# A row softmax over 4096 x 32768 values: the hardware loop turned by half a step

## The chip, the cores and the metric

One core of a Trainium2 chip. The time is that of one execution on the device in microseconds (us); lower is better. Medians are over several executions, and kernels of one comparison ran in turn on the same chip. Engines are named as in the profile: DVE is the vector engine, ACT the scalar engine, SP the sync engine (here it issues every transfer), PE the matrix engine (idle here); SPq and PEq are the instruction streams of SP and PE. In the kernels before and after, L75 and L83 are the lines of the file that issue a load and a store, and L115 is the first work of a tile, the max.

## The reference, cut to what matters

```python
logits = randn(16, 256, 32768).astype(float32); temperature = 1.0
scaled = logits / temperature
scaled = scaled - scaled.max(axis=-1, keepdims=True)
e = exp(scaled)
return e / e.sum(axis=-1, keepdims=True)          # float32
```

4096 rows of 128 KiB are read once and written once: 537 MB each way.

## The kernel before

Each row is cut in two halves on two neighbouring partitions, so a tile is 128 half rows of 16384 values (8.39 MB), and there are 64 tiles. Three tile buffers are used in turn. `normalise` does all arithmetic of a tile in place (four pieces of 4096 columns: max on DVE, exp on ACT, then the scaling on both). There is one chunk per tile (C = 1), and `turn` is None outside the loop. A step is one tile: normalise tile i, store it, load tile i+2 into the buffer that tile i-1 has left. Steps 0 to 2 are written out, steps 3 to 59 are a hardware loop of 19 turns of three steps, steps 60 to 63 are written out.

```python
_BUFS = 3                       # G = n_chunks = 64, C = 1
# ... cut: load, store, combine, pieces, normalise ...
    def step(i, turn=None, per_turn=0):
        g, c = divmod(i, C)
        end = turn is None and g == G - 1
        if c == 0:
            normalise(g, _END_PIECE if end else _PIECE)
        store(i, _END_DMA if end else CW, turn, per_turn)
        j = i + _BUFS - 1
        if i and j < n_chunks:
            end = turn is None and j // C == G - 1
            load(j, _END_DMA if end else CW, turn, per_turn)

    per_turn = 3
    first = per_turn
    turns = (n_chunks - (_BUFS - 1) - C - first) // per_turn      # 19
    with tc.manual_schedule():
        for i in range(_BUFS):
            load(i, _END_DMA if i < C else CW)
        for i in range(first):
            step(i)
        with tc.For_i(0, turns, 1, iteration_sync="reg_based") as turn:
            for i in range(first, first + per_turn):
                step(i, turn, per_turn)
        for i in range(first + turns * per_turn, n_chunks):
            step(i)
```

Of the kernel before, what the change touches and what calls it, by code (L numbers as in the profile page):

```python
# [11 lines left out]
_PIECE = 4096  # L12
_END_DMA = 4096
_END_PIECE = 4096
# [5 lines left out]
def kernel(  # L20
# [20 lines left out]
    C = W // CW  # L41
# [3 lines left out]
    G = N * _SPLIT // P  # L45
# [17 lines left out]
    def spans(total: int, step: int) -> list[tuple[int, int]]:  # L63
        return [(s, min(step, total - s)) for s in range(0, total, step)]

    def rows(i: int, turn, per_turn: int):
        g = i // C
        if turn is None:
            return slice(g * P, (g + 1) * P)
        return bass.ds(turn * (per_turn // C * P) + g * P, P)  # L70

    def load(i: int, step: int, turn=None, per_turn: int = 0) -> None:
        c = i % C
        for s, n in spans(CW, step):
            nc.sync.dma_start(  # L75
                out=buf[i % _BUFS][:, s : s + n],
                in_=x[rows(i, turn, per_turn), c * CW + s : c * CW + s + n],
            )

    def store(i: int, step: int, turn=None, per_turn: int = 0) -> None:  # L80
        c = i % C
        for s, n in spans(CW, step):
            nc.sync.dma_start(  # L83
                out=o[rows(i, turn, per_turn), c * CW + s : c * CW + s + n],
                in_=buf[i % _BUFS][:, s : s + n],
            )

    def combine(v, op) -> None:
        for j in range(n_rounds):
            mask = [i ^ (1 << j) for i in range(32)]  # L90
            nc.vector.stream_shuffle(  # L91
                out=v[:, j + 1 : j + 2], in_=v[:, j : j + 1], mask=mask
            )
            nc.vector.tensor_tensor(  # L94
                out=v[:, j + 1 : j + 2],
                in0=v[:, j : j + 1],
                in1=v[:, j + 1 : j + 2],
                op=op,
            )

    def pieces(g: int, step: int):
        k = 0
        for c in range(C):
            xs = buf[(g * C + c) % _BUFS]
            for s, n in spans(CW, step):
                yield k, xs[:, s : s + n], n
                k += 1

    def normalise(g: int, step: int) -> None:
        st = stat[g % _SETS]  # L110
        K = W // step
        nm, ssum, ee, f, ttj = (st[k][:, :K] for k in ("nm", "ssum", "ee", "f", "ttj"))
        nMh, Sh, rS = st["nMh"], st["Sh"], st["rS"]
        for k, xc, n in pieces(g, step):
            nc.vector.tensor_reduce(  # L115
                out=nm[:, k : k + 1], in_=xc, axis=X, op=A.max, negate=True
            )
            if inv_t != 1.0:
                nc.vector.tensor_scalar_mul(
                    out=nm[:, k : k + 1], in0=nm[:, k : k + 1], scalar1=inv_t  # L120
                )
            nc.scalar.activation(  # L122
                out=xc,
                in_=xc,
                func=Exp,
                bias=nm[:, k : k + 1],
                scale=inv_t,
                accum_out=ssum[:, k : k + 1],
            )
        nc.vector.tensor_reduce(out=nMh[:, 0:1], in_=nm, axis=X, op=A.min)  # L130
        combine(nMh, A.min)
        nc.scalar.activation(  # L132
            out=ee, in_=nm, func=Exp, bias=nMh[:, n_rounds : n_rounds + 1], scale=-1.0
        )
        nc.vector.tensor_tensor_reduce(  # L135
            out=ttj,
            in0=ee,
            in1=ssum,
            scale=1.0,
            scalar=0.0,  # L140
            op0=A.mult,
            op1=A.add,
            accum_out=Sh[:, 0:1],
        )
        combine(Sh, A.add)
        nc.vector.reciprocal(out=rS, in_=Sh[:, n_rounds : n_rounds + 1])  # L146
        nc.vector.tensor_scalar_mul(out=f, in0=ee, scalar1=rS)  # L147
        for k, xc, n in pieces(g, step):
            cut = int(n * _DVE_SHARE) // 512 * 512
            nc.vector.tensor_scalar_mul(  # L150
                out=xc[:, :cut], in0=xc[:, :cut], scalar1=f[:, k : k + 1]
            )
            nc.scalar.activation(  # L153
                out=xc[:, cut:], in_=xc[:, cut:], func=Copy, scale=f[:, k : k + 1]
            )

    def step(i: int, turn=None, per_turn: int = 0) -> None:
        g, c = divmod(i, C)
        end = turn is None and g == G - 1
        if c == 0:  # L160
            normalise(g, _END_PIECE if end else _PIECE)
        store(i, _END_DMA if end else CW, turn, per_turn)
        j = i + _BUFS - 1
        if i and j < n_chunks:
            end = turn is None and j // C == G - 1
            load(j, _END_DMA if end else CW, turn, per_turn)

    per_turn = 3
    first = per_turn
# [3 lines left out]
    with tc.manual_schedule():  # L173
        for i in range(_BUFS):
            load(i, _END_DMA if i < C else CW)
        for i in range(first):
            step(i)
        with tc.For_i(0, turns, 1, iteration_sync="reg_based") as turn:
# [4 lines that stand above are left out]
# [35 lines left out]
```

## Time and profile before

| | before |
|---|---|
| time, median of 4 runs | 2520.2 us (2519.25 to 2520.98) |
| span of the profiled run | 2519.8 us |
| DVE busy, ACT busy | 63%, 54% |
| transfer queue, share of 16 engines | 98.6% |
| GB/s inside the loop (200 to 2300 us) | 434 |
| GB/s in slice 38 of 40 | 224 |
| DVE's wait at the barrier of the loop's exit | 49.3 us |

How to read it: the row that is near 100% is the transfer queue (98.6%; the engines are at 63% and 54%), so I take an engine's idle time here to matter only where it holds up a transfer. The place to look for is where the rate falls, and there is one, just before the end. The profile's lines on it stand in the prediction.

### The profile page before, as it was taken

The numbers are of one execution on the slowest core, as the hardware profiler recorded it, in microseconds if no ns is written. First come the engines' busy times: TensorE is split into PE (matmuls) and PEld (weight loads), VectorE is DVE, ScalarE is ACT, GpSimd is POOL, SyncE is SP. The second block draws the span as 40 slices with busy tenths as digits, with TensorE's granted clock in tenths as the row PEclk, the third lists the DMA queues.
The fourth block names the chain that finished last, engine by engine and source line by source line (L and its number), as shares of the span: only waits on it lengthen the run. The fifth ranks groups of instructions, "written<-read, shape, count | busy, mean of one in ns | idle before, by whom it ended". The sixth has DMA issues, their size and how long they took to land. (4 is left out here: it accounts for less than half of the span.)

```text
span 2519.8 us, 4389 instructions
## 1 busy us (share of the span) xinstructions
DVE 1579.6 (63%) x1216; ACT 1368.7 (54%) x833; POOL 0.2 (0%) x4
## 2 busy tenths in 40 slices
DVE  6576565665766656657666666576566665765375
ACT  5464554655645546456455465464554654645255
POOL 0000000000000000000000000000000000000000
DMA  9999999999999999999999999999999999999599
GB/s 416 433 433 433 429 435 431 432 428 432 433 437 436 433 433 434 433 433 433 435 434 435 434 438 435 433 434 433 433 433 434 435 436 433 435 436 436 224 398 402
DMA packets 19733, 1073.79 MB, mean 426 GB/s; under 512 B 2192, under 2 KB 2192, under 8 KB 2192
## 3 DMA queue, kind: packets, MB, share of 16 engines
q1 hardware_dynamic: 19728, 1073.75, 98.6%
q14 instruction: 5, 0.04, 0.0%
HBM read 536.87 MB, written 536.87 MB: 426 GB/s over the span
## 5 line engine op out<-in xcount | busy, mean ns | idle before, releaser
L115 DVE TENSOR_REDUCE nm<-x 128x1 f32<-128x4096 f32 x256 | 1113.7, 4412 | 677.0 <-DMA x<-in_logits_dram 627.7
L122 ACT ACTIVATE x<-x,nm 128x4096 f32<-128x4096 f32 x256 | 949.2, 3708 | 1047.7 <-DVE nm L115 1033.0
L153 ACT ACTIVATE x<-x,f 128x1536 f32<-128x1536 f32 x256 | 382.3, 1564 | 73.5 <-DVE f L147 73.5
L150 DVE TENSOR_SCALAR x<-x,f 128x2560 f32<-128x2560 f32 x256 | 380.2, 1548 | 2.3
L135 DVE CUSTOM_DVE_ANT_0 ttj<-ee,ssum 128x4 f32<-128x4 f32 x64 | 10.4, 163 | 222.4 <-ACT ee L132 222.4
L122 ACT ACTIVATION_READ_ACCUMULATOR x<-x,nm 128x1 f32 x256 | 47.7, 186 | 0.0
L132 ACT ACTIVATE ee<-nm,nMh 128x4 f32<-128x4 f32 x64 | 18.0, 282 | 0.0
L147 DVE TENSOR_SCALAR f<-ee,rS 128x4 f32<-128x4 f32 x64 | 14.7, 229 | 2.2
L146 DVE RECIPROCAL rS<-Sh 128x1 f32<-128x1 f32 x64 | 10.5, 164 | 2.2
L94 DVE TENSOR_TENSOR nMh<-nMh 128x1 f32<-128x1 f32 x64 | 10.2, 159 | 2.2
L94 DVE TENSOR_TENSOR Sh<-Sh 128x1 f32<-128x1 f32 x64 | 10.2, 159 | 2.2
L130 DVE TENSOR_REDUCE nMh<-nm 128x1 f32<-128x4 f32 x64 | 10.0, 157 | 2.2
L91 DVE STREAM_SHUFFLE Sh<-Sh 128x1 f32<-128x1 f32 x64 | 9.7, 151 | 0.0
L91 DVE STREAM_SHUFFLE nMh<-nMh 128x1 f32<-128x1 f32 x64 | 9.7, 151 | 0.0
L122 ACT ACT_TABLE_LOAD x1 | 1.3, 1283 | 8.2 <-DMA x<-in_logits_dram 8.2
L135 DVE DVE_READ_ACCUMULATOR2_ANT Sh<- 128x1 f32 x64 | 5.3, 82 | 0.0
L91 DVE LOAD_MASK_SELECT nMh<-nMh x64 | 0.9, 14 | 2.8
L91 DVE LOAD_MASK_SELECT Sh<-Sh x64 | 0.9, 14 | 2.8
L199 POOL MEMSET const-bfloat16-1.0<- 128x1 bf16 x1 | 0.1, 103 | 0.0
L199 POOL MEMSET const-uint8-127<- 128x1 uint8 x1 | 0.1, 101 | 0.0
L199 POOL MEMSET const-float32-0.0<- 128x1 f32 x1 | 0.1, 99 | 0.2 <-issue 0.2
L199 POOL MEMSET const-float32-1.0<- 128x1 f32 x1 | 0.1, 99 | 0.0
## 6 DMA issues: line engine op xcount, KB each, us to landing
x<-in_logits_dram SPq DMA_DIRECT2D x8, 2048.0 KB, 29.4
out_dram<-x SPq DMA_DIRECT2D x4, 2048.0 KB, 15.8
out_dram<-x SPq DMA_DIRECT2D x63, 29.3
x<-in_logits_dram SPq DMA_DIRECT2D x62, 48.0
```

The lines of the kernel that those rows point to most:

```text
L91: nc.vector.stream_shuffle(out=v[:, j + 1 : j + 2], in_=v[:, j : j + 1], mask=mask)
L94: nc.vector.tensor_tensor(out=v[:, j + 1 : j + 2], in0=v[:, j : j + 1], in1=v[:, j + 1 : j + 2], op=op,)
L115: nc.vector.tensor_reduce(out=nm[:, k : k + 1], in_=xc, axis=X, op=A.max, negate=True)
L122: nc.scalar.activation(out=xc, in_=xc, func=Exp, bias=nm[:, k : k + 1], scale=inv_t, accum_out=ssum[:, k : k + 1],)
L130: nc.vector.tensor_reduce(out=nMh[:, 0:1], in_=nm, axis=X, op=A.min)
L132: nc.scalar.activation(out=ee, in_=nm, func=Exp, bias=nMh[:, n_rounds : n_rounds + 1], scale=-1.0)
L135: nc.vector.tensor_tensor_reduce(out=ttj, in0=ee, in1=ssum, scale=1.0, scalar=0.0, op0=A.mult, op1=A.add, accum_out=Sh[:, 0:1],)
L146: nc.vector.reciprocal(out=rS, in_=Sh[:, n_rounds : n_rounds + 1])
L147: nc.vector.tensor_scalar_mul(out=f, in0=ee, scalar1=rS)
L150: nc.vector.tensor_scalar_mul(out=xc[:, :cut], in0=xc[:, :cut], scalar1=f[:, k : k + 1])
L153: nc.scalar.activation(out=xc[:, cut:], in_=xc[:, cut:], func=Copy, scale=f[:, k : k + 1])
L199: nc = _bacc.Bacc("TRN2", target_bir_lowering=False, num_devices=1)
```

## The change

Intent: after the loop only stores and loads should be left to issue at once, not a normalisation that they all wait for. The body of a step is the same, cut at another place: store i, load i+2, normalise i+1. The first tile is normalised ahead of all steps.

```diff
     def step(i: int, turn=None, per_turn: int = 0) -> None:
         g, c = divmod(i, C)
         end = turn is None and g == G - 1
-        if c == 0:
-            normalise(g, _END_PIECE if end else _PIECE)
         store(i, _END_DMA if end else CW, turn, per_turn)
         j = i + _BUFS - 1
         if i and j < n_chunks:
             end = turn is None and j // C == G - 1
             load(j, _END_DMA if end else CW, turn, per_turn)
+        if c == C - 1 and g + 1 < G:
+            end = turn is None and g + 1 == G - 1
+            normalise(g + 1, _END_PIECE if end else _PIECE)
 ...
         for i in range(_BUFS):
             load(i, _END_DMA if i < C else CW)
+        normalise(0, _PIECE)
         for i in range(first):
             step(i)
```

## The prediction

> **What bounds the kernel now.** I read the page first. Of its 2519.8 us the vector engine is busy 63% and the scalar engine 54%; the one transfer queue is at 98.6%. The slices show how even that is, and where it is not: in 40 slices of 63.0 us (2519.8 / 40) the rate is about 433 GB/s, but slice 38, which covers 2330.8 to 2393.8 us, has 224.
>
> ```profile
> DMA  9999999999999999999999999999999999999599
> GB/s 416 433 433 433 429 435 431 432 428 432 433 437 436 433 433 434 433 433 433 435 434 435 434 438 435 433 434 433 433 433 434 435 436 433 435 436 436 224 398 402
> q1 hardware_dynamic: 19728, 1073.75, 98.6%
> ```
>
> So the kernel is bound by its transfers, with one hole near the end. Second I asked for busy times by stretch around that hole.
>
> ```profile
> 200.00:2300.00 2100.00, 1339.83 (x1028) 1157.53 (x704) 0.00 (x0) 1.00 1.00 434
> 2321.50:2369.50 48.00, 0.00 (x0) 0.00 (x0) 0.00 (x0) 1.00 0.88 381
> 2369.50:2398.10 28.60, 24.80 (x20) 21.36 (x13) 0.00 (x0) 1.00 0.00 0
> 2398.10:2519.80 121.70, 73.74 (x57) 64.10 (x39) 0.00 (x0) 1.00 0.98 414
> ```
>
> The columns are the stretch, its length, busy time of the vector, scalar and GpSimd engines with instructions in brackets, clock, transfer share and GB/s. For 48 us data moves and nothing is computed; then for 28.6 us one tile is computed and no byte moves; then both run again. The two stretches ought to lie on top of each other. Third, the transfers issued around it, from the sync engine's timeline, and the waits of both sides in that stretch (total, times, longest):
>
> ```profile
> 2320.35 0.34 SPq L83 DMA_DIRECT2D out_dram<-x  x1
> 2320.90 0.35 SPq L75 DMA_DIRECT2D x<-in_logits_dram  x1
> 2398.10 0.34 SPq L83 DMA_DIRECT2D out_dram<-x  x1
> 2398.49 0.42 SPq L75 DMA_DIRECT2D x<-in_logits_dram  x1
> 2426.46 0.34 SPq L83 DMA_DIRECT2D out_dram<-x  x1
> ```
> ```profile
> SPq L178 <- DMA x<-in_logits_dram: 28.0, 2, 19.3
> SPq L178 <- DMA out_dram<-x: 19.3, 1, 19.3
> DVE nm L115 <- PEq L213: 49.3, 1, 49.3
> ```
>
> Line 178 is the loop. At 2321.5 us the sync engine has issued the last store and load of the last turn (tiles 59 and 61; there are 64, one chunk each, and the 19 turns cover 3 to 59). It then waits 28.0 + 19.3 = 47.3 us for every transfer the loop issued to land, to 2369.0, and only then does a barrier of all engines let anyone past. Tile 60 landed early in that time, but its normalisation is the first thing behind the barrier: the vector engine idles 49.3 us and begins at 2369.53. The sync engine's next instruction, store 60, needs that normalisation, and load 62 stands behind it in program order. That is the hole. The chain that ended last starts there too:
>
> ```profile
> 2369.53 17.41 DVE nm L115 x4
> ...
> 2393.58 4.50 ACT x L153 x3
> 2398.10 0.34 SPq L83
> 2398.44 0.05 issue
> 2398.49 42.61 DMA x<-in_logits_dram
> 2441.10 0.02 issue
> 2441.12 17.41 DVE nm L115 x4
> ```
>
> From load 62's issue 42.61 us pass until it lands and tile 62 starts; 2519.8 - 2398.1 = 121.7 us from store 60's issue to the end.
>
> [...]
>
> **The change, part by part.** A turn was normalise i, store i, load i+2; it becomes store i, load i+2, normalise i+1.
> 1. Work: 64 normalisations, 64 stores, 64 loads before and after. The built programs agree: order and shapes on the vector and scalar engines are unchanged, and the sync engine issues the same transfers in the same order. Only the cut moves: those two engines enter the loop after tile 3 and leave it after tile 60. Cost 0.
> 2. Inside the loop: stretched over turns the stream is the same, so what released each wait stays (52 waits of the vector engine for a load between 300 and 2300 us, 535.5 us, so 10.3 us of slack per tile). Cost 0. The first store of the first turn now waits also for a normalisation from outside the loop, which it depended on anyway.
> 3. Entry: I see no barrier there in the trace (tile 2's store is issued at 99.04, load 4 at 101.78, and the transfer share stays at 0.97 or more from 100 to 190 us). Cost 0.
> 4. Exit: the sync engine's wait for load 61 does not depend on the change: load 61 needs store 58 to have landed, not tile 60. It still ends at 2369.0. Tile 60 is now normalised inside the loop: it starts when load 60 lands. In the loop that comes about 10 us after the previous load's issue (150.36 to 159.75, 188.99 to 198.81), so at about 2331, and takes 28.6 us (the stretch above), to about 2360. That is 9 us before the sync engine is free, so it is hidden.
> 5. Behind the barrier: store 60 has nothing to wait for. The vector engine began 0.5 us after the wait's end (2369.53); I give the sync engine until 2369.7. Store 60 moves from 2398.10 to 2369.7: -28.4 us. Load 62 follows by 0.4 us as before, and tile 61 starts at 2369.5 instead of 2397.90: the same 28.4 us.
> 6. The rest: at store 60 the state is then that of before, shifted: queues empty, tile 61 landed, its normalisation just starting. So the same 121.7 us follow. 2369.7 + 121.7 = 2491.4 us of span; the timed median is 0.4 above the span (2520.17 against 2519.8), so 2491.8 us. That is 28.4 / 2520.2 = 1.1% less.
>
> **Rivals.** (a) The barrier is left later: the drain now follows tile 60, not 59. If tile 60 ended after 2369.0, its overrun would be added. Against it: 9 us of margin, and in the loop a normalisation runs beside transfers all the time. It would have to take 37 us, not 28.6. (b) The first transfer behind the barrier starts late[...]. For it: nothing measured. Against it: the vector engine started 0.04 us after the barrier's release[...].[...] (c) The hole is hidden anyway, because the tail is bound by its own computation. Then little would come of it and the time would stay near 2515. Against it: the chain runs through store 60 and load 62's landing, and the tail moves six tiles of 8.39 MB (four stores, two loads) = 50.3 MB, which at 434 GB/s take 116 of its 121.7 us; it is bound by transfers and cannot have taken in the hole. (d) More than the hole closes: the share falls already at about 2363.6, where the 18.3 MB left at 2321.5 (381 GB/s x 48 us) would be through at 434 GB/s. Those 5.4 us to landing, with barrier and refill, stay: the sync engine still waits for the landing.
>
> **Range and chances.** The sum has one term, and its size is read off directly: 28.4 us. The lower end allows for a tail 3 us shorter; the upper for rival (b) and a little of (a). 2488.5 to 2496. To be faster by over 2% the time would have to be under 2470, that is 50 us less, nearly twice the hole; to be slower by 2%, over 2570. Neither has a mechanism: 1% each for what I have overlooked, 98% within 2%.
>
> **What would show it.** Right: the slice at 224 GB/s rises to about 400; the transfer issues behind the exit come 49 us after the last in the loop, not 77; the vector engine works from about 2331 to 2360, and its 49.3 us wait for the barrier shrinks to about 10; the distance from the first store behind the exit to the end stays near 121.7 us. Wrong: if that distance grows (something in the tail relied on the lead), if the first store is issued over 1 us after the landing of load 61 (b), if the exit moves later (a), or if any turn in the loop got longer than the 117 us that three tiles take (three spacings of 39.0 us, from 188.42 to 227.40).

Cut from the record are a paragraph of general statements about the hardware that no trace of this case shows and, in rival (b), a mechanism and the size given to it. No term of the sum was among them: it is 2520.2 - 28.4 = 2491.8 us (the span 2369.7 + 121.7 = 2491.4, and 0.4 to the timed median). The upper end of the range, 2496, held an allowance of 3 us for rival (b), which was a guess of mine. The transfer share is 0.00 from 2369.5 to 2398.1 us, and a compare-and-branch of the loop's line takes 49 ns on SP and ACT and 61 ns on DVE (medians of 20), so 19 of them are 0.9 to 1.2 us in all, where the sync engine waits 2173.7 us for DVE before its stores (67 waits) and DVE 10.3 us for each load. That nothing is to be won in the loop, at 434 GB/s, was not shown.

## The result, and the profile after

The changed kernel took 2491.44 us (median of 4 runs, 2490.77 to 2492.46) against 2520.2 us; ratio 0.9886, 95% interval 0.9869 to 0.9904. Ratios are the mean time of one kernel's fast runs over the mean of the other's of the same rounds, so not quite the ratio of the medians quoted. The gain is clear of the noise, but below 2%.

The page of the changed kernel, the same three lines as before (rate by slice, then the queue with its packets, MB and share of 16 engines):

```profile
DMA  9999999999999999999999999999999999999999
GB/s 421 421 438 433 426 433 435 425 437 437 431 433 435 435 433 436 432 435 432 438 431 436 433 436 437 430 436 433 437 428 437 433 438 429 436 433 432 426 405 404
q1 hardware_dynamic: 19728, 1073.75, 99.9%
```

The slice at 224 is gone: slice 38 has 426. Busy time by stretch of the changed kernel (stretch, length, DVE, ACT, GpSimd, clock, transfer share, GB/s), cut at the same events as before:

```profile
200.00:2300.00 2100.00, 1341.68 (x1029) 1158.78 (x705) 0.00 (x0) 1.00 1.00 434
2319.50:2367.50 48.00, 24.68 (x19) 21.37 (x13) 0.00 (x0) 1.00 0.93 401
2367.50:2367.90 0.40, 0.07 (x1) 0.00 (x0) 0.00 (x0) 1.00 0.00 0
2367.90:2489.50 121.60, 73.88 (x57) 64.10 (x39) 0.00 (x0) 1.00 0.98 414
```

The two stretches that ought to lie on top of each other do now. The 48 us of the drain hold one tile's worth of computing (24.68 us of DVE, against none before), the stretch without transfers has shrunk from 28.6 to 0.4 us, and what follows is as long as before (121.6 us against 121.7). The loop runs at 434 GB/s in both.

The sync engine's transfers around the exit, and the waits of both sides there (total, times, longest), changed kernel:

```profile
2318.55 0.34 SPq L83 DMA_DIRECT2D out_dram<-x  x1
2319.10 0.35 SPq L75 DMA_DIRECT2D x<-in_logits_dram  x1
2367.91 0.34 SPq L83 DMA_DIRECT2D out_dram<-x  x1
2368.30 0.42 SPq L75 DMA_DIRECT2D x<-in_logits_dram  x1
2396.40 0.34 SPq L83 DMA_DIRECT2D out_dram<-x  x1
```
```profile
SPq L180 <- DMA x<-in_logits_dram: 28.2, 2, 19.3
SPq L180 <- DMA out_dram<-x: 19.3, 1, 19.3
DVE nm L115 <- PEq L215: 10.7, 1, 10.7
```

From store 59 to store 60 it is 49.4 us instead of 77.8. The sync engine's own wait at the exit is the same (28.2 + 19.3 = 47.5 us against 47.3); only what stands behind it changed. DVE's wait at the barrier fell from 49.3 to 10.7 us: tile 60 was done that much before the barrier opened.

The chain that ended last, changed kernel, begins with the transfers and no longer with a normalisation:

```profile
2367.91 0.34 SPq L83
2368.30 42.40 DMA x<-in_logits_dram
2410.72 17.41 DVE nm L115 x4
```

### The profile page after: what moved, and what is told of

It is laid out like the page before. It is cut to its first block, busy times and chain, and to the rows that moved or that the text cites. A ratio compares the mean times of both kernels' runs of the same rounds, so it can differ in the third digit from the quotient of the medians.

```text
span 2489.5 us, 4388 instructions
## 1 busy us (share of the span) xinstructions
DVE 1579.6 (63%) x1216; ACT 1368.7 (55%) x833; POOL 0.2 (0%) x4
## 3 DMA queue, kind: packets, MB, share of 16 engines
q1 hardware_dynamic: 19728, 1073.75, 99.9%
## 5 line engine op out<-in xcount | busy, mean ns | idle before, releaser
L115 DVE TENSOR_REDUCE nm<-x 128x1 f32<-128x4096 f32 x256 | 1113.7, 4412 | 646.6 <-DMA x<-in_logits_dram 635.9
L94 DVE TENSOR_TENSOR nMh<-nMh 128x1 f32<-128x1 f32 x64 | 10.2, 159 | 2.2
L94 DVE TENSOR_TENSOR Sh<-Sh 128x1 f32<-128x1 f32 x64 | 10.2, 159 | 2.2
## 6 DMA issues: line engine op xcount, KB each, us to landing
x<-in_logits_dram SPq DMA_DIRECT2D x8, 2048.0 KB, 29.3
out_dram<-x SPq DMA_DIRECT2D x63, 29.3
```

The lines of the kernel that those rows point to most:

```text
L94: nc.vector.tensor_tensor(out=v[:, j + 1 : j + 2], in0=v[:, j : j + 1], in1=v[:, j + 1 : j + 2], op=op,)
L115: nc.vector.tensor_reduce(out=nm[:, k : k + 1], in_=xc, axis=X, op=A.max, negate=True)
```

## The experiments

Theory A is the prediction's: the gain is one normalisation (28.6 us) that stood between the exit's barrier and the next store, nothing else. Rival B: the turns themselves got cheaper, 28.8 / 19 = 1.5 us each. Rival C: the order of the three parts matters in every step. Rival D: the more of a step lies before the exit, the better. (The prediction's own rivals are (a) to (d), in small letters.)

**Two states, first.** Over all rounds the kernel before falls into two groups: of its 48 runs (the first four included) 19 lie between 2518.5 and 2521.0 us (mean 2520.1), 27 between 2536.8 and 2542.0 (mean 2539.7), two at 2531 and 2533. The granted clock (that of PE, idle here) is 1.00 in every run for which the record lists it. I call them the quick and the lazy state (the later expectations say faster and slower; the first ones were written before they were known) and compare within one. Averages over both are what makes most ratios' intervals wide (about 0.4% each way).

### The changed kernel again, in two later sessions

> The changed kernel once more, as the yardstick on this chip. Both theories: 28.8 us less than before, so about 2491.4 us.

> The changed kernel on one more chip, for how often each of its two states comes and for the next line's yardstick: 2491 us in the faster state, 2509 in the slower; in the same state 28.8 to 29.5 less than before (2520, 2539).

Measured: 2509.35 us median (2490.78 to 2513.42), ratio 0.9894; and 2506.56 us (2491.05 to 2511.72), ratio 0.988. With the first four runs there are 16: six between 2490.8 and 2492.5 (mean 2491.3), ten between 2505.5 and 2513.4 (mean 2509.2). In the quick state the change is worth 2520.05 - 2491.32 = 28.7 us, in the lazy one 2539.66 - 2509.23 = 30.4 us. So the states are not of the change's making, and its gain is the same in both within their spread. My first expectation gave one time and missed the lazy state; the second gave both.

Where the lazy state loses its time is seen by the same stretch of the first repeat, which was in it:

```profile
200.00:2300.00 2100.00, 1332.74 (x1026) 1153.76 (x702) 0.00 (x0) 1.00 1.00 431
```

It is 431 GB/s in the loop instead of 434, and the loss does not begin with the run: from 200 to 700 us both traces read 433, later the quick one 434 and the lazy one 429 to 431. Store 59 is issued at 2335.55 us instead of 2318.55: 17.0 of the 17.7 us by which the spans differ arise in the loop. In the quick run stores follow each other in a nearly fixed pattern (about 38.5, 38.5, 39.0 us in the later turns), in the lazy one they wander between 38.5 and 40.0.

### No loop at all

```diff
-        with tc.For_i(0, turns, 1, iteration_sync="reg_based") as turn:
-            for i in range(first, first + per_turn):
-                step(i, turn, per_turn)
-        for i in range(first + turns * per_turn, n_chunks):
+        for i in range(first, n_chunks):
             step(i)
```

> All 64 steps written out in the order of before, no hardware loop. Theory A (the gain is the normalisation that stood behind the loop's exit barrier): without a loop there is no barrier, so the order of before does no harm; the whole hole goes, the part that the change leaves too (the changed kernel's transfer share in 2360 to 2370 us is short by 0.21 x 5 + 0.50 x 5 = 3.5 us), so 2491.4 - 3.5 = about 2488 us, and no slice under 400 GB/s. Rival B (the gain comes per turn, some 1.5 us in each of 19 turns, from cheaper turns): also loses all loop costs, so it too allows 2488, and may be lower; it can't tell A from B but gives the size of what the exit still costs. Rival C (the order of normalise, store and load matters everywhere): as slow as before, about 2520.

> The kernel without a loop again. It was seen only in the slower state, 2.4 us under the changed kernel there. If the faster state exists without a loop: about 2488 us in it, so 3 to 4 us under the changed kernel; if all six runs are again at 2505 to 2512, the faster state is rarer or absent without a loop, and the changed kernel is the better one where it is in its faster state.

Measured: 2507.89 us (2505.86 to 2511.97), ratio 0.9899; and 2508.95 us (2497.17 to 2511.69), ratio 0.9887. Eleven of twelve runs are in the lazy state (mean 2508.9), one is at 2497.17 between the groups. Rival C falls: the order of before, without a loop, is as fast as the changed kernel in that state, 31 us under the kernel it is copied from. But the 3.5 us by which I expected it to be faster do not show in the time (2508.9 against 2509.2). The traces show where they are; stores 59 and 60 in the trace of `unrolled`:

```profile
2340.10 0.33 SPq L83 DMA_DIRECT2D out_dram<-x  x1
...
2379.46 0.33 SPq L83 DMA_DIRECT2D out_dram<-x  x1
```

That step takes 39.4 us, like one inside a loop. From store 59 to the end the kernel without a loop takes 2508.8 - 2340.10 = 168.7 us, the changed kernel in the same state 2507.2 - 2335.55 = 171.7: it does save 3.0 us at the exit. In the traces of `unrolled_second` and `after_third` it is 168.1 against 171.7. What it saves there it has lost before: both its traces reach store 59 later (2340.1 and 2341.8 us) than both lazy traces of the changed kernel (2335.6 and 2333.0). Whether that is chance in this state, or a small cost of the program without a loop, two traces of each do not show. My 2488 us was wrong because it was built on the quick state, which this kernel never clearly reached; why it does not is open. (The 2.4 us in the second expectation is 2.0 by the means of that session's lazy runs.)

### Two exits instead of one

Both orders, with nine turns, three steps written out, nine turns:

```diff
-        with tc.For_i(0, turns, 1, iteration_sync="reg_based") as turn:
+        half = turns // 2
+        second = first + (half + 1) * per_turn
+        with tc.For_i(0, half, 1, iteration_sync="reg_based") as turn:
             for i in range(first, first + per_turn):
                 step(i, turn, per_turn)
-        for i in range(first + turns * per_turn, n_chunks):
+        for i in range(first + half * per_turn, second):
+            step(i)
+        with tc.For_i(0, half, 1, iteration_sync="reg_based") as turn:
+            for i in range(second, second + per_turn):
+                step(i, turn, per_turn)
+        for i in range(second + half * per_turn, n_chunks):
             step(i)
```

> The order of before with two loops of 9 turns and three steps written out between them: two exits, 18 turns instead of 19. Theory A: one more hole of 28.6 us and the 3.5 us that an exit costs anyway, so 2520 + 32 = about 2552 us, and a second slice pair near half rate in the middle. Rival B: about 2520 or slightly less, as there is one turn fewer.

> The changed order with the same two loops. Theory A: one more exit costs only the 3.5 us of drain and refill, so about 2495 us; the gap to the two-loop kernel in the old order is 57 us, twice that of the change. Rival B: about 2491 to 2493, the gap stays at 28 us or less.

Measured: 2564.46 us (2561.96 to 2566.38), ratio 1.0118, and 2509.88 us (2506.23 to 2511.83), ratio 0.9908. The gap between the orders is 54.6 us: it has nearly doubled with the number of exits while there is one turn fewer. Rival B needs it to stay at 28 and falls. Against the lazy state of the kernels with one loop the second exit costs 2564.5 - 2539.7 = 24.8 us in the old order (32 expected) and 2509.9 - 2509.2 = 0.7 us in the new (3.5 expected). Both are too small, by some 7 and 3 us, and again the traces are cleaner than the times. The middle exit in the sync engine's timeline, first the old order, then the new: the last store in the first loop and the two behind it.

```profile
1164.24 0.34 SPq L83 DMA_DIRECT2D out_dram<-x  x1
...
1242.77 0.34 SPq L83 DMA_DIRECT2D out_dram<-x  x1
...
1271.13 0.34 SPq L83 DMA_DIRECT2D out_dram<-x  x1
```
```profile
1159.12 0.34 SPq L83 DMA_DIRECT2D out_dram<-x  x1
...
1208.45 0.34 SPq L83 DMA_DIRECT2D out_dram<-x  x1
...
1236.94 0.34 SPq L83 DMA_DIRECT2D out_dram<-x  x1
```

The step over the exit is 78.5 us in the old order and 49.3 in the new; the next is 28.4 and 28.5, the one after (to 1314.45 and 1280.07) 43.3 and 43.1. The three together are 150.2 and 120.9 us, where three steps before the exit take 117 (39.0 each) in the old order and 116 (38.7 each) in the new. So an exit in mid-stream costs 33 us in the old order and 4 to 5 us in the new, and the difference, 29.3 us, is again one normalisation. Most of what is missing in the times is in the traces too: these runs were not lazy throughout, so the lazy state is not quite their yardstick. In the new order store 29, the last of the first loop, comes at 1159.1 us, as in the quick run of the changed kernel (1158.8) and not as in its first lazy one (1164.2). In the old order the steps from store 32 to 59 take 1051.1 us, against 1056.8 in the one lazy trace of that order with one loop (`before_60` below). So a run need not keep one state to its end; what sets it is open.

### The loop turned by another half step

A turn loads, normalises and stores, so that store 60 also lies before the exit:

```diff
-        if c == 0:
-            normalise(g, _END_PIECE if end else _PIECE)
-        store(i, _END_DMA if end else CW, turn, per_turn)
         j = i + _BUFS - 1
         if i and j < n_chunks:
             end = turn is None and j // C == G - 1
             load(j, _END_DMA if end else CW, turn, per_turn)
+        if i + 1 < n_chunks:
+            end = turn is None and g + 1 == G - 1
+            normalise(g + 1, _END_PIECE if end else _PIECE)
+            store(i + 1, _END_DMA if end else CW, turn, per_turn)
 ...
+        normalise(0, _PIECE)
+        store(0, CW)
         for i in range(first):
```

> The turn moved by another half step: a turn loads, computes and stores, so that the store of tile 60 is issued inside the loop and only a load is left to issue first at the exit. Theory A (what counts is how long the queue is empty around the barrier): the exit now waits for store 60 to land too, issued at about 2357 us and landed at about 2387; load 62 then runs alone for some 20 us while tile 61 is only being normalised, so the queue is empty about 6.5 us at the barrier and about 10 us after load 62 landed, 13 us more than in the changed kernel: about 2500 to 2506 us. Rival D (the more of a step is done before the exit, the better): 2491 or less. Rival B (per turn): 2491.

Measured: 2509.08 us median, ratio 0.9887: two runs in the quick state (2499.43, 2500.32) and two in the lazy one (2517.84, 2519.55). Against the changed kernel in the same state (in the other sessions; it did not run in this one) that is 8.6 and 9.5 us more. Rival D falls. The profiled run was a lazy one; its transfers behind tile 60's store, and the busy time in the two stretches where it matters:

```profile
2375.70 0.34 SPq L83 DMA_DIRECT2D out_dram<-x  x1
2405.58 0.35 SPq L75 DMA_DIRECT2D x<-in_logits_dram  x1
2434.19 0.34 SPq L83 DMA_DIRECT2D out_dram<-x  x1
```
```profile
2395.00:2400.00 5.00, 0.00 (x0) 0.00 (x0) 0.00 (x0) 1.00 0.39 170
2400.00:2405.00 5.00, 0.00 (x0) 0.00 (x0) 0.00 (x0) 1.00 0.12 52
...
2425.00:2430.00 5.00, 2.74 (x9) 3.85 (x5) 0.00 (x0) 1.00 0.03 13
2430.00:2435.00 5.00, 5.00 (x4) 4.17 (x3) 0.00 (x0) 1.00 0.00 0
```

The sizes in the expectation are estimates: 2357 is where tile 60's work ends in the changed kernel (2357.1 us), a store lands 29.3 us after its issue there (the page's median), and a tile's 8.39 MB at 434 GB/s are 19.3 us. Here load 62, issued at 2405.58 us, ran alone to about 2425: the share is 0.97 to 1.03 from 2405 to 2425 us and 0.03 in the 5 us behind. There are the two holes expected: at the exit, which now waits for store 60 as well, and after load 62 has landed alone, while tile 61 is still being normalised. By share they are some 7 and 10 us. The time lost is less, because not all of the exit's hole is new and because part is made good later. From store 59 to store 61 this run takes 98.1 us, against 78.3 in the first lazy trace of the changed kernel; from there to the end it takes 81.8 against 93.3, with load 62 landed already: 8.2 us more in sum. The 2499.9 us of the quick state lie just below the 2500 to 2506 expected; the 13 us by which I had it above the changed kernel were too many by about 4.

### More work in the tile behind the barrier

First with additional work in each third tile, in both orders: the first max-reduction of tiles 3, 6, ... 60 is done three times.

```diff
         for k, xc, n in pieces(g, step):
+            for _ in range(2 if k == 0 and g % 3 == 0 and 0 < g < G - 1 else 0):
+                nc.vector.tensor_reduce(
+                    out=nm[:, k : k + 1], in_=xc, axis=X, op=A.max, negate=True
+                )
             nc.vector.tensor_reduce(
```

> The order of before, with the first max-reduction of each third tile (3, 6, ... 60, not 0 and 63) done three times instead of once: 2 x 4.41 = 8.8 us more of vector work in those 20 tiles, the result unchanged. In the loop it fits the 10.3 us that the vector engine idles per tile. Theory A: only tile 60 counts, whose normalisation stands between the barrier and store 60: +8.8 us, about 2529. Rival B, or a tail bound by itself: +0 (hidden), or if the loop feels it, up to +176.

> The changed order with the same extra work. Theory A: tile 60 ends at 2357.1 us and the wait for load 61 at 2367.3, so 10.2 us of margin take in 8.8: +0, about 2491.4. If the margin is not there (rival a of the prediction, the exit waits for the compute engines): up to +8.8, 2500. The two kernels with the extra work should differ by 28.8 + 8.8 = about 37.6 us.

Measured: 2582.36 us (2581.0 to 2583.63), ratio 1.0186 (interval 1.0154 to 1.0219, across the 2% line, so "unclear" by the record), and 2546.0 us (2544.47 to 2548.31), ratio 1.0043. The gap between the two is 36.4 us, as expected (37.6). But both are some 53 to 55 us slower than expected of them: the loop does feel the work. Its three steps take 41.3 + 48.0 + 29.8 = 119.1 us instead of 38.5 + 38.5 + 39.0 = 116.0 in the changed kernel, and 19 times 3.1 is 59. My premise was wrong: the 10.3 us in which DVE idles before each tile are not slack of the same size for the queue. The reason was not shown.

At the exit the premise of the experiment does hold. From the last store in the loop to the first behind it the old order now takes 87.0 us (77.8 + 9.2), the new 50.0 (49.4 + 0.6), and in the new order DVE's wait at the barrier shrinks from 10.7 to 2.2 us (its lines are L119 and L219, as four lines were added above them):

```profile
DVE nm L119 <- PEq L219: 2.2, 1, 2.2
```

So the margin that the prediction claimed was there and took in the 8.8 us nearly in full.

Then the same work in tile 60 alone, which leaves the loop as it was:

```diff
         if c == 0:
-            normalise(g, _END_PIECE if end else _PIECE)
+            normalise(g, _END_PIECE if end else _PIECE, i == n_chunks - 4)
```

(In `normalise`, this last argument adds the two max-reductions of the first piece, as above.)

> The order of before with 8.8 us of additional max-reduction in tile 60 alone, the tile behind the barrier (the kernel with the extra work in each third tile had slowed the loop as well, which I had not expected). Theory A: +8.8 us on each state of before: about 2529 where before reads 2520, about 2548 where before reads 2539; the distance from the last store in the loop to the first behind it 77.8 + 8.8 = 86.6 us. A rival in which that normalisation is hidden beside something: +0.

Measured: three runs in the quick state (2527.67, 2528.72, 2528.89; mean 2528.4) and three in the lazy one (2541.80, 2546.77, 2549.91; mean 2546.2); ratio over both 1.0029, interval 0.9982 to 1.0076. In the quick state that is 8.8 us more than the 2519.7 us of the kernel before in the same rounds, where 2 x 4.41 = 8.8 was put in; in the lazy state it is 2546.2 - 2539.3 = 6.9, from three runs spread over 8 us. In the sync engine's timeline (of a lazy run) the last store and load in the loop, and the first store behind it:

```profile
2339.50 0.34 SPq L83 DMA_DIRECT2D out_dram<-x  x1
2340.05 0.35 SPq L75 DMA_DIRECT2D x<-in_logits_dram  x1
2426.20 0.34 SPq L83 DMA_DIRECT2D out_dram<-x  x1
```

From store to store it is 86.7 us (86.6 expected), against 77.8 in the kernel before. Work put between the barrier and the store is paid in full, which is theory A turned round.

### A try at something better: loads in four pieces

```diff
-            end = turn is None and j // C == G - 1
-            load(j, _END_DMA if end else CW, turn, per_turn)
+            load(j, _END_DMA, turn, per_turn)
 ...
-            load(i, _END_DMA if i < C else CW)
+            load(i, _END_DMA)
```

and the same without a loop.

> A try at a version that beats both: the changed kernel with every load cut into four pieces of 2 MB, as its first and last loads already are. Hypothesis E (the states of 2491 and 2509 us differ because a store is issued only some 10 us before the queue would run dry[...]): a tile's first piece lands some 10 us or more before its last, the normalisation starts and ends earlier, stores are issued earlier, and every run is at 2491 or a few us less. Hypothesis F (the slower state is slower transfers, whatever is queued): two states as before, 2491 and 2509.

> The kernel without a loop, with loads in four pieces. Hypothesis E: no exit and no run-dry, so about 3.5 us under the kernel with the loop and pieces, some 2488 us. Hypothesis F: 2505 to 2512 as the kernel without a loop was in all its six runs, or 2488 in the other state.

Measured: 2506.81 us (2506.02 to 2507.35), ratio 0.9918, and 2501.49 us (2501.37 to 2501.86), ratio 0.9898. (The 10 us of hypothesis E are the changed kernel's: a store goes out when DVE ends a tile, and from there DVE waits 533.3 / 52 = 10.3 us for the next load.) The pieces did land one after the other: in the trace of `after_pieces` DVE waits for 241 of the 256 (616.6 us), and where it waits for a tile's last piece, that piece landed at least three max-reductions, 3 x 4.41 = 13.2 us, after the first. In the changed kernel it waits 64 times (635.9 us). Neither hypothesis fits. The two states do not show here (all twelve runs lie within 1.4 us of their kernel's others), but what is left is not the quick one: the loop runs at 432 GB/s in its later three quarters, and the queue has 46512 packets instead of 19728 for the same bytes (323 transfers instead of 137, at 144 packets each). With the loop out of the way another 5.3 us go. So there is a version whose runs all come in at 2501.5 us, but none that beats the changed kernel in its quick state (2491.3); over the 16 runs seen of the changed kernel, in both states, the mean is 2502.5, so the two are about equal on average.

## Why the prediction was right

**The hole** (steps 4 and 5). The one term of the sum, 28.4 us, is the step over the exit: 77.8 us became 49.4. It is shown by the trace, it doubles with a second exit, and it grows by 8.8 when 8.8 us of work are put there.

**Nothing in the loop** (steps 1 to 3). 434 GB/s in both traces between 200 and 2300 us, and the sum of DVE's waits for loads between 300 and 2300 us is 533.3 us against 535.5. The two-loop kernels exclude a gain per turn.

**The margin** (step 4). Tile 60 was worked on from 2328.67 to 2357.1 us, predicted 2331 to 2360; the exit's wait ended at 2367.3, so 10.2 us of margin where I had 9. Rival (a) did not come. Of rival (b), the late first transfer, nothing came either: store 60 was issued 0.6 us after that, where I had 0.7.

**The tail** (step 6). 121.6 us against 121.7. Rival (c), a tail bound by its own computation, is excluded by this and by the kernel with the longer tile 60.

**Rival (d)**, what the exit still costs: predicted to stay, with 5.4 us of thin transfers as its size, and it did; 3 to 5 us by the traces of the kernel without a loop and the kernel with two.

Two sizes were off and cancelled. The exit came at 2367.3 us, not 2369.0, because this run's loop was 1.8 us shorter: store 59 at 2318.55 instead of 2320.35. And I added 0.4 us from the span to the timed median, mixing the median of the timed runs with the span of another run; within one run the distance is 1.84 us in both kernels (2521.64 against 2519.8, 2491.34 against 2489.5). So the hit within 0.4 us on the time is luck; the 28.4 us are not.

Two readings of mine are loose, and nothing rests on them. The paragraph that is cut had the sync engine at the barrier while the share was 0.00; from 2369.5 to 2398.1 us it no longer stood there but at store 60's own wait for the normalisation (28.5 us). At the barrier the transfer share had fallen to 0.61 (2360 to 2365 us) and 0.09 (2365 to 2370). And the 37 us of rival (a) should be 2369 - 2331 = 38.

What the prediction did not know is the second state. The range of 2488.5 to 2496 holds for the session that it was measured in, all of whose runs were quick; in the two later sessions ten of twelve runs of the same kernel took 2505 to 2514 us. That the session was a quick one was luck for the range. The difference between the kernels holds in both states, the absolute time does not.

## What to carry to other kernels

In every trace whose waits at the exit were read, the sync engine stood there for transfers that the loop had issued: 47.3 us before the change and 47.5 after, with no byte moving behind either wait (share 0.00), 47.3 to 48.1 us in the kernels with two exits, `before_60` and `after_plus2`, 28.5 in `turned_further` and 52.9 in `after_pieces`. So look at what stands behind the barrier: it should be transfers that can be issued at once, and the work that they depend on should be done during the drain (49.4 us from store 59 to store 60 instead of 77.8). Cutting a turn too late is also wrong: here a store in the drain lengthened it, left the next load alone on the queue and cost 9 us. Before comparing two versions to a fraction of a per cent, look whether the runs of one kernel fall into groups, and compare within a group or by distances inside the trace.
